# A hybrid decoder layer on one core: the merge's first two blocks interleaved, one gate half moved into attention, the sums of the down projection behind its weights

## The chip, the cores and the metric

The kernel runs on one core of one Trainium2 chip. The metric is the device time of one execution in microseconds (us). The engines are TensorE (PE for its matmuls, PEld for its weight loads), VectorE (DVE), ScalarE (ACT), GpSimd (POOL) and SyncE (SP, which here only issues DMAs; a few stores are issued on ACT's queue). Each engine runs its own instructions in a fixed order, so an instruction that waits holds everything behind it on that engine.

## What is computed

One decoder layer on x of 1024 positions x 1024 channels in float32, and a last norm:

```python
xn = rmsnorm(x, norm_mix_w)
da_q, da_k, da_v, sw_q, sw_k, sw_v, g_da, g_sw = split_cols(xn @ w_in)
y_da = diff_attention(da_q, da_k, da_v, lam, lam_init, subln_w)
y_sw = sliding_window_attention(sw_q, sw_k, sw_v, sinks)
merged = sigmoid(g_da) * (y_da @ w_br_da) + sigmoid(g_sw) * (y_sw @ w_br_sw)
x = x + merged @ w_mix_out
xn = rmsnorm(x, norm_ffn_w)
x = x + conv_ffn(xn, w_up, conv_w, conv_b, w_down)
return rmsnorm(x, norm_final_w)
```

`conv_ffn` is an up-projection to 2 x 2816 channels, a causal depthwise convolution of width 3, a SwiGLU and a down-projection. Differential attention has 4 heads of two 64-wide queries each, the sliding window (128 positions) 8 heads with sinks.

## The kernel before

Activations are held transposed: channels on the 128 partitions, positions along the free axis, in 8 tiles of 128 channels (KC = 8), the positions in two halves of 512 (H2). Every float32 operand of a product is split into a high part (a cast to fp32r on ACT, `wh`, `yh`, `mh`, `h`) and the rest (a subtraction on DVE, `wl`, `yl`, `ml`); a product is three matmuls, high x high, low x high and high x low, which are lines L153 to L155 in the helper `mm3`. Weights come in blocks of 128 output channels: `load_w` loads one (SP), casts it (L132, ACT) and subtracts (L134, DVE). `next_w` keeps two weights prepared ahead; there are three raw buffers (RAW = 3).

The order of the instructions on each engine is set by a scheduler from the program; `tc.high_priority` moves what is inside it forward, and `tc.issue_after(i)` keeps what is inside it behind the instruction i.

The stages, with their place in the profile:

- `project` (to some 247 us): the columns of `w_in` for queries, keys and values.
- `attention` (to some 488 us): six units u of eight steps of 128 queries. Units 0 to 3 are a head of differential attention each, units 4 and 5 are half of the sliding window's heads (`sw_step`). A step computes scores (L707), the softmax on DVE, ACT and DVE (L714, L716, L721), transposes (L728), a split of the transposed weights (L731 on ACT, L732 on DVE) and the product with the values, "the AV matmuls" (L738). It then copies half of the result across partitions (L740, ACT) and adds the other half (L745, DVE) into `ys`, which is stored to `yd` (L540, ACT's queue).
- Gates. The columns of `w_in` for the two gates do not belong to attention, but their matmuls fill PE between its steps. `back_half(m, hf)` does one half (512 positions) of one gate tile: 24 matmuls into a psG buffer (of two), a copy to SBUF (L548, ACT) and a store to `gd` (L549, ACT's queue). HALVES says how many halves follow which step: one tuple before attention, one for each unit, and a last one for those left over, which `rest` puts between the splits of y.
- `rest`: loads the eight tiles of y from `yd` (L763, four buffers) and splits them (L806 on ACT, L807 on DVE), with the gate halves left over between them; then the merge, 502.45 to 589.5 us. For each block m of 128 output channels: load the gate tiles of both branches (L775), multiply by the norm's factor (L776, POOL), sigmoid (L783, ACT), 24 matmuls of the differential branch into `sc`, 2 x 12 of the sliding window's into two psG buffers, DVE multiplies the gates in (L787, L792), POOL adds the branches (L793, on DVE for the last block), and the sum is split into `mh` (L796, ACT) and `ml` (L797, DVE). There are four buffers `gr` for gate tiles, two for each block, so the gate loads of block m + 2 wait for block m.
- `mix`, `hidden`: the output product of the merge, the norm, the up-projection, convolution and SwiGLU; the results c of 22 tiles go to `hd` in DRAM.
- `down` (from some 1106 us): the product with `w_down`. First 16 "pieces" over tiles 0 to 5 of the hidden channels; then a Strassen-Winograd scheme over tiles 6 to 13 with operands B11, B21, B22 and the sums T1 to T4; then tiles 14 to 21. In the scheme, step m of the first loop takes the weight of block m and multiplies it with B11 and B21 (24 matmuls, L887); the second loop multiplies the sums of weights S1 to S4 and A22 with T1, T2, B22, T3, T4. `sums_h(k)` makes the k-th tile of T1 to T4: four loads `hr` (L980), four subtractions on DVE (L996, L998, L999, L1002) and four splits (L806, L807). It has nine buffers `hr`.

Names that recur below: S is the start of the merge's first matmul; "DA(m)" and "SW(m)" are the matmuls of the two branches of block m.

Of the kernel before, what the change touches and what calls it, by code (L numbers as in the profile page):

```python
# [17 lines left out]
P = 128  # L18
D = 1024
T = 1024  # L20
KC = D // P
# [10 lines left out]
LPAD, RPAD = 480, 480  # L32
LAM_INIT = 0.2

HALVES = ((2,), (0, 0, 0, 0, 1, 0, 1, 0), (0, 0, 0, 0, 1, 0, 1, 0), (0, 0, 0, 0, 1, 0, 1, 0), (0, 0, 0, 1, 1, 0, 1, 0), (1, 0, 1, 0, 1, 0, 1, 0), (0, 0, 1, 0, 1, 0, 1, 0), (4,))
NEGMASK = 1e30


# [4 lines left out]
class Trunk:  # L43
# [652 lines left out]
    def sw_step(self, g, n, st):  # L696
        nc, ap = self.nc, self.ap
        q, k = st
        k0 = max(n - 1, 0) * P
        w = P if n == 0 else 256  # L700
        bo = T + (P if n == 0 else 0)
        sc = self.tl(self.psS, [P, 4, 256], "sc")
        s = self.tl(self.st, [P, 4, 4], "sw", bufs=4)
        L = self.tl(ap, [P, 4, 256], "L", bufs=4)
        for h in range(4):
            for part in range(2):
                nc.tensor.matmul(sc[:, h, :], q[h][:, n * P:(n + 1) * P], k[part][:, k0:k0 + 256], start=part == 0, stop=part == 1)  # L707


        a, at, we = (0, w, w + 1) if n == 0 else (1, 0, w)  # L710
        nc.gpsimd.tensor_copy(L[:, :, at:at + 1], self.nsink[:, 4 * g:4 * g + 4].unsqueeze(2))
        for h in range(4):
            slope, ns = 2.0 ** -(4 * g + h + 1), self.nsink[:, 4 * g + h:4 * g + h + 1]
            nc.vector.tensor_tensor_reduce(L[:, h, a:w], sc[:, h, a:w], self.bias[:, bo + a:bo + w], slope, ns, ALU.add, ALU.min, s[:, 0, h:h + 1])  # L714
        for h in range(4):
            nc.scalar.activation(L[:, h, :we], L[:, h, :we], AF.Exp, bias=s[:, 0, h:h + 1], scale=-1.0, accum_out=s[:, 2, h:h + 1])  # L716
        nc.vector.reciprocal(s[:, 3, :], s[:, 2, :])
        if n:
            nc.gpsimd.memset(L[:, :, 0:1], 0.0)
        for h in range(4):  # L720
            self.last = nc.vector.tensor_scalar(L[:, h, a:w], L[:, h, a:w], s[:, 3, h:h + 1], None, ALU.mult)  # L721
        po = self.tl(self.psT, [P, H2], "t")
        nblk = w // P
        parts = []
        for b in range(nblk):
            ps = self.tl(self.psT, [P, 4, P], "t")
            for h in range(4):
                nc.tensor.transpose(ps[:, h, :], L[:, h, b * P:(b + 1) * P], self.ident)  # L728
            pt = self.tl(ap, [P, 2, 4, P], "aT", F32R, bufs=5)
            hi, lo = pt[:, 0], pt[:, 1]  # L730
            nc.scalar.copy(hi, ps)  # L731
            nc.vector.tensor_tensor(lo, ps, hi.bitcast(F32), ALU.subtract)  # L732
            parts.append((hi, lo))
        for b, (hi, lo) in enumerate(parts):
            kb = k0 // P + b
            va = self.vsw[kb // 4][:, kb % 4, g]
            for m, pt in enumerate((hi, lo)):
                nc.tensor.matmul(po, va, pt, start=b == 0 and m == 0, stop=b == nblk - 1 and m == 1)  # L738
        t = self.tl(self.gpool, [P, 4, P], "g", bufs=2)[0:64]
        nc.scalar.copy(t, po[64:128].rearrange("p (h q) -> p h q", h=4))  # L740
        pv = po[0:64].rearrange("p (c e q) -> p c e q", c=2, e=2)
        tv = t.rearrange("p (c e) q -> p c e q", e=2)
        y = self.tl(ap, [P, 2, P], "ys", bufs=3)
        for e in range(2):
            nc.vector.tensor_tensor(y[64 * e:64 * e + 64], pv[:, :, e], tv[:, :, e], ALU.add)  # L745
        self.store(self.yd[4 + 2 * g:6 + 2 * g, :, n * P:(n + 1) * P].rearrange("c p q -> p c q"), y)


    def rest(self, gctx):
        nc, tc = self.nc, self.tc  # L750
        with ExitStack() as ctx:
            e = ctx.enter_context
            mctx = ExitStack()
            mh, ml = [], []
            with gctx, ExitStack() as bctx:
                yrp = bctx.enter_context(tc.tile_pool(name="yrp", bufs=4, reuse_waits="tile"))
                yp = bctx.enter_context(tc.tile_pool(name="yp", bufs=1, reuse_waits="tile"))
                bp = bctx.enter_context(tc.tile_pool(name="bp", bufs=2, reuse_waits="tile"))
                parts = []
                for c in range(8):  # L760
                    with tc.high_priority(200):
                        r = self.tl(yrp, [P, T], "yr")
                        nc.sync.dma_start(r, self.yd[c])  # L763
                    parts.append(self.split(*(yp.tile([P, T], F32R, name=f"y{p}{c}") for p in "hl"), r))
                    if self.back[7][0]:
                        self.back_half(*self.back[7][0].pop(0))
                yact = [lambda kc, hf, o=o: [t[:, hf * H2:(hf + 1) * H2] for t in parts[o + kc]] for o in (0, 4)]
                self.xctx.close()
                mp = mctx.enter_context(tc.tile_pool(name="mp", bufs=1, side="right", reuse_waits="tile"))
                for m in range(KC):  # L770
                    w = self.next_w()
                    gs = []
                    for br in range(2):
                        g = self.tl(bp, [P, T], "gr", bufs=4)
                        nc.sync.dma_start(g, self.gd[8 * br + m])  # L775
                        i = nc.gpsimd.tensor_tensor(g, g, self.rstd, ALU.mult)  # L776
                        if m == 0:

                            tc.add_manual_dep(i.ins, self.last.ins.name, mybir.DependencyInfo(mybir.DependencyClass.Sync, mybir.DependencyReason.DATA),
                                              reason="softmax first")  # L780

                        with tc.issue_after(self.hi.ins) if br else nullcontext():
                            nc.scalar.activation(g, g, AF.Sigmoid)  # L783
                        gs.append(g)
                    ps = self.tl(self.psS, [P, T], "sc")
                    self.mm3_both(ps, w, yact[0], range(4))
                    nc.vector.tensor_tensor(gs[0], gs[0], ps, ALU.mult)  # L787
                    for hf in range(2):
                        ps = self.tl(self.psG, [P, H2], "g")
                        self.mm3(ps, w, yact[1], hf, range(4), o=4)  # L790
                        g = gs[1][:, hf * H2:(hf + 1) * H2]
                        nc.vector.tensor_tensor(g, g, ps, ALU.mult)  # L792
                    (nc.vector if m == KC - 1 else nc.gpsimd).tensor_tensor(gs[0], gs[0], gs[1], ALU.add)  # L793
                    a = mp.tile([P, T], F32R, name=f"mh{m}")
                    b = mp.tile([P, T], F32R, name=f"ml{m}")
                    nc.scalar.copy(a, gs[0])  # L796
                    nc.vector.tensor_tensor(b, gs[0], a.bitcast(F32), ALU.subtract)  # L797
                    mh.append(a)
                    ml.append(b)

            pair = self.mix(mh, ml, mctx)
            self.hidden(pair)
            self.down()
# [231 lines left out]
    def down(self):  # L1035

        nc, tc = self.nc, self.tc
        with ExitStack() as ctx:
# [28 lines left out]
            sums = [lambda k=k: self.sums_h(k) for k in range(4)]  # L1067
            pss = {}
            n = N1 // 2
            for i, (m, c) in enumerate(self.pieces):  # L1070
# [3 lines left out]
                w = [v[:, i % 2 * n:i % 2 * n + n] for v in w2]  # L1074
# [17 lines left out]
                if i in STORE:  # L1092

                    with tc.issue_after(self.load.ins):
                        self.late.pop(0)()
                if i == len(self.pieces) - 1:
                    sums.pop(0)()
                if c == 1:

                    for hf in range(m < 4, 2):  # L1100
# [3 lines left out]
            ys = []  # L1104
            for m in range(4):
                wh, wl = self.next_w()
                y, ps = bank(1), pss[m, 0]
                ys.append(y)
                self.product(y, (wh[:, 0:4], wl[:, 0:4]), "B11", skip=True, low=True)
                self.product(ps, (wh[:, 4:8], wl[:, 4:8]), "B21", first=False)  # L1110
                for p in (y, ps):
                    tt(col(m, 0), col(m, 0), p, ALU.add)
                if sums:
                    sums.pop(0)()
            late = [(hf, j) for hf in range(2) for j in range(N1 + 8, NF)]
            for m, y in enumerate(ys):
                w = self.next_w()
# [36 lines left out]
            for hf in range(2):  # L1154
                for m in range(KC if hf == 0 else KC - 2):
                    w = self.next_w()
# [10 lines left out]
            for a, b in ((0, q), (q, H2)):  # L1167
                for m, w in ws:
                    ps = bank(m % 2)[:, :q]
                    mms(ps, w, 1, js, a, b, lambda n, m=m: tail.pop(0)() if a and n == (4 if m < KC - 1 else 2) else None)  # L1170
                    sq = evac(ps, m, 1, a, b)
# [100 lines left out]
```

## Time and profile before

| | us |
|---|---|
| median of 3 runs | 1345.15 (1344.61 to 1345.49) |
| profiled execution | 1344.88 |
| its span | 1343.0 |
| TensorE busy | 1326.8 |
| VectorE busy | 1052.5 |
| ScalarE busy | 602.3 |
| GpSimd busy | 488.8 |

The mean granted clock of TensorE was 0.997 of full speed. The profile is of one execution. Its page gives each engine's busy time as a share of the span; other views list what an engine waited for, the busy time of each engine in given stretches, and every instruction with its start, its length and, in brackets, the idle time of its engine ahead of it and what ended that. L12 is line 12 of the kernel. Matmuls are pipelined: the length shown for one is longer than the distance to the next.

### The profile page before, as it was taken

What the parts mean: (1) busy time and instruction counts of PE and PEld (TensorE: products, weight loads), DVE (VectorE), ACT (ScalarE), POOL (GpSimd) and SP (SyncE); (2) the same over time, 40 slices, a digit from 0 to 9 for tenths busy, and PEclk for the clock granted to TensorE, in tenths of its full rate; (3) what the DMA queues carried; (4) which work ended last, traced back from release to release, by engine and by line L of the source; (5) the groups of instructions that cost most, each with busy time, mean ns of one, the idle gap of its engine ahead of it and who ended that gap; (6) DMA issues with size and microseconds to landing.
All of it is one profiled execution on the core that took longest, in us unless ns stands there. A gap on an engine that the chain in (4) does not pass through costs nothing.

```text
span 1343.0 us, 17167 instructions
## 1 busy us (share of the span) xinstructions
PE 1326.8 (99%) x6304; PEld 1105.7 (82%) x6304; DVE 1052.5 (78%) x1425; ACT 602.3 (45%) x929; POOL 488.8 (36%) x364
## 2 busy tenths in 40 slices
PE   8999999999999999999999999999999999999997
PEld 6888888888888878888888888888888888788886
DVE  7846775388898976445669999999999998967454
ACT  8432232276667774344444434343434345432433
POOL 0346652000101016642446566666666611131011
PEclk9999999999999999999999999999999999999998
DMA  7244443966554245324522222222222239642342
GB/s 258 108 146 162 148 149 119 273 170 189 143 148 144 70 155 206 141 95 130 167 79 95 79 79 85 88 79 79 88 85 80 86 128 320 220 145 98 94 141 79
DMA packets 63812, 179.49 MB, mean 134 GB/s; under 512 B 7024, under 2 KB 16880, under 8 KB 63728
## 3 DMA queue, kind: packets, MB, share of 16 engines
q1 hardware_dynamic: 52272, 161.22, 36.8%
q10 hardware_dynamic: 11456, 17.18, 3.5%
q8 instruction: 50, 0.82, 0.2%
q14 instruction: 34, 0.28, 0.1%
HBM read 129.61 MB, written 48.76 MB: 133 GB/s over the span
## 4 chain that ended last, share of the span: by engine, by line
PE 72%; DVE 15%; issue 8%; DMA 2%; ACT 1%; POOL 1%; SPq 0%; POOLq 0%; DVEq 0%; ACTq 0%
PE t L887 24%; PE g L153 4%; PE g L154 4%; PE g L155 4%; DVE c L1031 3%; PE y L1056 3%; PE d L1056 3%; PE sc L154 3%; PE sc L155 3%; PE sc L153 3%; PE d L887 3%; PE sc L619 3%; PE y L887 2%; DVE wl L113 2%; DMA hr<-hd 2%
## 5 line engine op out<-in xcount | busy, mean ns | idle before, releaser
L1020 POOL TENSOR_TENSOR us<-us,rstd 128x1024 f32<-128x1024 f32 x42 | 92.6, 2225 | 85.0 <-DVE us L452 47.6
L1029 ACT ACTIVATE c<-us,vecs 128x1024 f32<-128x1024 f32 x44 | 54.8, 1248 | 118.3 <-POOL us L1020 113.8
L132 ACT CAST wh<-raw 128x1024 fp32r<-128x1024 f32 (+2 forms) x58 | 58.7, 1012 | 107.9 <-PE sc L154 35.8
L134 DVE TENSOR_TENSOR wl<-raw,wh 128x1024 fp32r<-128x1024 f32 (+2 forms) x58 | 78.3, 1352 | 32.5 <-ACT wh L132 22.8
L113 DVE TENSOR_TENSOR sl<-sf,sh 128x1024 fp32r<-128x1024 f32 x62 | 89.3, 1442 | 12.8 <-ACT sh L111 12.8
L111 ACT CAST sh<-sf 128x1024 fp32r<-128x1024 f32 x62 | 64.5, 1042 | 61.6 <-PE t L887 44.0
L97 POOL TENSOR_TENSOR sf<-rv 128x512 f32<-128x512 f32 x30 | 51.3, 1711 | 93.6 <-DVE sl L113 51.1
L1031 DVE SCALAR_TENSOR_TENSOR c<-us,vecs,c 128x1024 f32<-128x1024 f32 x44 | 75.4, 1746 | 2.7 <-ACT c L1029 2.7
L99 POOL TENSOR_TENSOR sf<-raw,rv 128x512 f32<-128x512 f32 x30 | 56.7, 1891 | 46.3 <-DVE sl L113 46.3
L1032 DVE SCALAR_TENSOR_TENSOR c<-us,vecs,c 128x1024 f32<-128x1024 f32 x44 | 73.2, 1696 | 0.0
L153 PE MATMUL g<-xh,wh 128*128 128x512 f32 x176 | 71.0, 403 | 1.5 <-ACT g L548 1.5
L154 PE MATMUL g<-xl,wh 128*128 128x512 f32 x176 | 70.3, 400 | 0.0
L155 PE MATMUL g<-xh,wl 128*128 128x512 f32 x176 | 70.3, 399 | 0.0
L170 POOL TENSOR_TENSOR rs<-ms,mhalf 128x8 f32<-128x8 f32 (+2 forms) x9 | 13.5, 1499 | 155.5 <-DVE ms L168 149.4
L1012 ACT ACTIVATE c<-c 128x1024 f32<-128x1024 f32 x22 | 23.4, 1064 | 89.6 <-DVE c L1032 89.6
L113 DVE TENSOR_TENSOR wl<-raw,wh 128x1024 fp32r<-128x1024 f32 (+1 forms) x35 | 61.8, 1765 | 0.3 <-ACT wh L111 0.2
L602 POOL MEMSET aT<- 128x128 f32 x32 | 6.1, 204 | 151.5 <-PE t L648 101.2
L623 DVE CUSTOM_DVE_ANT_0 L<-sc,bias 128x128 f32<-128x128 f32 (+7 forms) x64 | 47.8, 752 | 16.6 <-PE sc L619 13.7
L98 POOL TENSOR_TENSOR sf<-sf,raw 128x512 f32<-128x512 f32 x31 | 58.2, 1877 | 2.2
L624 ACT ACTIVATE L<-L,sm 128x128 f32<-128x128 f32 (+7 forms) x64 | 49.6, 778 | 20.0 <-DVE sm L623 17.3
L776 POOL TENSOR_TENSOR gr<-gr,rstd 128x1024 f32<-128x1024 f32 x16 | 40.3, 2523 | 43.9 <-DMA gr<-gd 43.7
L113 DVE TENSOR_TENSOR wl<-rv,wh 128x512 fp32r<-128x512 f32 x30 | 54.0, 1800 | 2.6 <-ACT wh L111 2.6
(435 smaller groups left out, 4338.4 us busy)
## 6 DMA issues: line engine op xcount, KB each, us to landing
u<-qd SPq DMA_DIRECT2D x72, 256.0 KB, 6.4
raw<-in_w_down SPq DMA_DIRECT2D x27, 512.0 KB, 3.7
hr<-hd SPq DMA_DIRECT2D x50, 256.0 KB, 4.8
raw<-in_w_up SPq DMA_DIRECT2D x23, 512.0 KB, 3.5
raw<-in_w_in SPq DMA_DIRECT2D x22, 512.0 KB, 3.8
hd<-c SPq DMA_DIRECT2D x22, 512.0 KB, 2.6
rv<-in_w_up SPq DMA_DIRECT2D x21, 512.0 KB, 3.5
gr<-gd SPq DMA_DIRECT2D x16, 512.0 KB, 3.4
```

The lines of the kernel that those rows point to most:

```text
L111: cast = nc.scalar.copy(hi, src)
L113: low = nc.vector.tensor_tensor(lo, src, hi.bitcast(F32), ALU.subtract)
L132: self.hi = nc.scalar.copy(wh, raw)
L134: self.lo = (eng or nc.vector).tensor_tensor(wl, raw, wh.bitcast(F32), ALU.subtract)
L153: nc.tensor.matmul(ps, wh[:, kc + o, :], ah, start=first and n == 0, stop=False)
L154: nc.tensor.matmul(ps, wh[:, kc + o, :], al, start=False, stop=False)
L155: nc.tensor.matmul(ps, wl[:, kc + o, :], ah, start=False, stop=last and n == len(kcs) - 1)
L887: nc.tensor.matmul(ps, (ah, ah, al)[p][:, k, :], (bh, bl, bh)[p], start=first and n == p == 0, stop=last and p == 2 and n == len(ks) - 1, ...
L1020: i = (nc.vector if m % NF == 0 else nc.gpsimd).tensor_tensor(us[:, 2:], us[:, 2:], self.rstd, ALU.mult)
L1031: nc.vector.scalar_tensor_tensor(c, us[:, 1:T + 1], cw[1], c, ALU.mult, ALU.add)
L1032: nc.vector.scalar_tensor_tensor(c, us[:, 0:T], cw[0], c, ALU.mult, ALU.add)
L1056: nc.tensor.matmul(ps, v[:, n, :], x, start=n == i == 0, stop=n == len(js) - 1 and i == 2)
```

## The change

1. HALVES: one half gate more in unit 5 (after its first step), one less at the end (3 instead of 4).
2. `sw_step`: the tile that receives the copy L740 is no longer taken from the gates' pool (`gpool`, tag "g", two buffers, which the gate copies L548 use too) but from attention's own pool (tag "sq", one buffer, which `da_norm` uses for its squares).
3. The merge's loop body is cut in two: `first(m)` has the weight, the gates and DA(m) with L787, `second(m)` has SW(m) and everything after it. The calls run first(0), first(1), second(0), second(1), first(2), second(2), first(3) and so on.
4. `down`: `sums_h(0)` was called after the last piece, and `sums_h(k + 1)` after the products of step m = k. Now `sums_h(m)` is called in step m after `next_w`, ahead of the products, and is kept behind the cast of the weight that `next_w` prepared last (`self.hi`).

```diff
--- before.py
+++ after.py
@@ -32,7 +32,7 @@
 LPAD, RPAD = 480, 480
 LAM_INIT = 0.2
 
-HALVES = ((2,), (0, 0, 0, 0, 1, 0, 1, 0), (0, 0, 0, 0, 1, 0, 1, 0), (0, 0, 0, 0, 1, 0, 1, 0), (0, 0, 0, 1, 1, 0, 1, 0), (1, 0, 1, 0, 1, 0, 1, 0), (0, 0, 1, 0, 1, 0, 1, 0), (4,))
+HALVES = ((2,), (0, 0, 0, 0, 1, 0, 1, 0), (0, 0, 0, 0, 1, 0, 1, 0), (0, 0, 0, 0, 1, 0, 1, 0), (0, 0, 0, 1, 1, 0, 1, 0), (1, 0, 1, 0, 1, 0, 1, 0), (1, 0, 1, 0, 1, 0, 1, 0), (3,))
 NEGMASK = 1e30
 
 
@@ -736,7 +736,7 @@
             va = self.vsw[kb // 4][:, kb % 4, g]
             for m, pt in enumerate((hi, lo)):
                 nc.tensor.matmul(po, va, pt, start=b == 0 and m == 0, stop=b == nblk - 1 and m == 1)
-        t = self.tl(self.gpool, [P, 4, P], "g", bufs=2)[0:64]
+        t = self.tl(ap, [P, 4, P], "sq", bufs=1)[0:64]
         nc.scalar.copy(t, po[64:128].rearrange("p (h q) -> p h q", h=4))
         pv = po[0:64].rearrange("p (c e q) -> p c e q", c=2, e=2)
         tv = t.rearrange("p (c e) q -> p c e q", e=2)
@@ -767,7 +767,7 @@
                 yact = [lambda kc, hf, o=o: [t[:, hf * H2:(hf + 1) * H2] for t in parts[o + kc]] for o in (0, 4)]
                 self.xctx.close()
                 mp = mctx.enter_context(tc.tile_pool(name="mp", bufs=1, side="right", reuse_waits="tile"))
-                for m in range(KC):
+                def first(m):
                     w = self.next_w()
                     gs = []
                     for br in range(2):
@@ -785,6 +785,9 @@
                     ps = self.tl(self.psS, [P, T], "sc")
                     self.mm3_both(ps, w, yact[0], range(4))
                     nc.vector.tensor_tensor(gs[0], gs[0], ps, ALU.mult)
+                    return m, w, gs
+
+                def second(m, w, gs):
                     for hf in range(2):
                         ps = self.tl(self.psG, [P, H2], "g")
                         self.mm3(ps, w, yact[1], hf, range(4), o=4)
@@ -797,6 +800,13 @@
                     nc.vector.tensor_tensor(b, gs[0], a.bitcast(F32), ALU.subtract)
                     mh.append(a)
                     ml.append(b)
+
+                todo = []
+                for m in range(KC):
+                    todo.append(first(m))
+
+                    while len(todo) > (m == 0):
+                        second(*todo.pop(0))
 
             pair = self.mix(mh, ml, mctx)
             self.hidden(pair)
@@ -1093,8 +1103,6 @@
 
                     with tc.issue_after(self.load.ins):
                         self.late.pop(0)()
-                if i == len(self.pieces) - 1:
-                    sums.pop(0)()
                 if c == 1:
 
                     for hf in range(m < 4, 2):
@@ -1104,14 +1112,15 @@
             ys = []
             for m in range(4):
                 wh, wl = self.next_w()
+
+                with tc.issue_after(self.hi.ins):
+                    sums.pop(0)()
                 y, ps = bank(1), pss[m, 0]
                 ys.append(y)
                 self.product(y, (wh[:, 0:4], wl[:, 0:4]), "B11", skip=True, low=True)
                 self.product(ps, (wh[:, 4:8], wl[:, 4:8]), "B21", first=False)
                 for p in (y, ps):
                     tt(col(m, 0), col(m, 0), p, ALU.add)
-                if sums:
-                    sums.pop(0)()
             late = [(hf, j) for hf in range(2) for j in range(N1 + 8, NF)]
             for m, y in enumerate(ys):
                 w = self.next_w()
```

## The prediction

> **What bounds the kernel now.** I read the table of engines first, then what TensorE (PE) waited for, then the stages of the edits.
>
> ```profile
> span 1343.0 us, 17167 instructions
> PE 1326.8 (99%) x6304; PEld 1105.7 (82%) x6304; DVE 1052.5 (78%) x1425; ACT 602.3 (45%) x929; POOL 488.8 (36%) x364
> PE t L280 <- ACT wh L310: 5.0, 1, 5.0
> PE g L153 <- ACT g L548: 1.5, 4, 0.5
> PE y L887 <- DVE wl L134: 0.5, 1, 0.5
> PE t L738 <- DVE aT L732: 0.4, 1, 0.4
> PE y L887 <- ACT wh L132: 0.3, 1, 0.3
> PE d L1083 <- DVE wl L134: 0.2, 1, 0.2
> PE t L728 <- DVE ys L745: 0.2, 1, 0.2
> ```
>
> The first two lines are the page's top, the rest the list of PE's waits (total us, times, longest). PE is busy 99% of the span: the kernel is bound by matmuls, and the change neither adds nor removes one. It can only win or lose waits, and those that it can reach are few. The biggest, 5.0 us, is at the kernel's start and not touched. The stages of the edits, by windows (us, PE busy, PEld, DVE, ACT, POOL busy, PEclk, DMA share, GB/s):
>
> ```profile
> 450.00:486.00 36.00, 34.40 (x187) 27.81 (x187) 33.46 (x106) 26.72 (x74) 1.96 (x9) 1.00 0.26 80
> 486.00:502.45 16.45, 16.45 (x74) 13.48 (x73) 9.50 (x9) 10.97 (x14) 4.80 (x2) 1.00 0.58 202
> 502.45:589.50 87.05, 87.05 (x386) 72.10 (x385) 44.79 (x39) 34.32 (x35) 57.90 (x21) 1.00 0.45 164
> 1164.00:1180.00 16.00, 15.24 (x67) 11.96 (x66) 15.90 (x25) 7.01 (x10) 0.00 (x0) 1.00 0.73 240
> ```
>
> The end of attention (to 486) has 36.00 - 34.40 = 1.60 us of idle PE, the start of the last part of `down` 0.76. The gates left over (to 502.45) and the merge (to 589.5) have none: there the change can only lose. The granted clock is 1.00 in all four.
>
> **What a wait costs.** Matmuls are pipelined, so a wait costs more than the idle time shown. From PE's timeline (start, length; in brackets the idle time ahead and what ended it):
>
> ```profile
> 411.36 0.50 PE L153 MATMUL g<-xh,wh 128*128 128x512 f32 x1 [0.25 <-ACT g L548]
> 411.69 0.39 PE L154 MATMUL g<-xl,wh 128*128 128x512 f32 x1
> 502.45 0.39 PE L153 MATMUL sc<-yh,wh 128*128 128x512 f32 x1
> 589.49 0.39 PE L153 MATMUL sc<-mh,wh 128*128 128x512 f32 x1
> ```
>
> The last two rows bound the merge: 8 blocks x 48 matmuls in 87.04 us, so 0.227 us from start to start, although each is shown 0.39 long. Idle time is thus counted only 0.16 us after the next could have started, and the first after a wait takes 0.33 instead of 0.23 (411.36 to 411.69). I add 0.26 us to each wait. A gate half of 24 matmuls is 5.44 us, a merge block 10.88.
>
> **Part 1: a half gate into the last unit, and tiles of its own.** A gate's matmuls (L153) need a psG buffer, which the ACT copy L548 empties. Rows of the timeline:
>
> ```profile
> 461.70 0.50 PE L153 MATMUL g<-xh,wh 128*128 128x512 f32 x1 [0.35 <-ACT g L548]
> 473.55 0.50 PE L153 MATMUL g<-xh,wh 128*128 128x512 f32 x1 [0.39 <-ACT g L548]
> 482.13 1.19 PE L738 MATMUL t<-aT,v 128*128 128x512 f32 x4 [0.37 <-DVE aT L732]
> 423.06 0.63 PE L728 MATMUL t<-ident,L 128*128 128x128 f32 x4 [0.18 <-DVE ys L745]
> 483.36 0.58 ACT L740 COPY g<-t 64x512 f32<-64x512 f32 x1 [1.52 <-PE t L738]
> 483.97 0.58 ACT L548 COPY g<-g 128x512 f32<-128x512 f32 x1
> 484.61 0.50 PE L153 MATMUL g<-xh,wh 128*128 128x512 f32 x1 [0.50 <-ACT g L548]
> 487.91 0.58 ACT L740 COPY g<-t 64x512 f32<-64x512 f32 x1 [1.51 <-DMA yd<-ys]
> ```
>
> At 483.36 the step's copy L740 waits 1.52 us for its AV matmul L738 (PE), with L548 queued behind it on ACT; PE then needs what L548 frees. The step's copy sits in the gates' own pool of two, so each can also wait for the other's consumer or store (the row at 487.91). With tiles of their own and one more half, the instruction order of the changed kernel puts each L548 of this stretch mostly ahead of the step's L740, at least 7 us of PE work (some 30 matmuls) before its buffer is used again. So the four waits should go: 0.25 + 0.35 + 0.39 + 0.50 + 4 x 0.26 = 2.5 us (bounds 0 to 2.5). The waits of L738 and L728 (0.37 + 0.18 + 2 x 0.26 = 1.07) have more gate matmuls to fill them, but DVE is busy 33.46 of 36.00 us here, so late DVE work may stay late: I take half, 0.5 (bounds 0 to 1.07). Part 1: -3.0. The new tile shares its one buffer with attention's squares; their last reader, the column sums after unit 3, precedes it in the order, and between steps only DVE's L745 holds it: nothing.
>
> The moved half takes its store L549 and the cast and split of its weight with it, on queues that precede the merge anyway. What it leaves is cover: after the last AV matmul 46 gate matmuls remain (10.4 us), 65 before (14.7). That cover hides the store of the last step and the reload and split of y, which the merge needs.
>
> **Part 2: merge's first two blocks together.** PE now runs DA(0), a part of SW(0), DA(1), the rest of SW(0), SW(1), then blocks as before. This answers the shorter cover: counting matmuls in the new order, the last y part is needed at S + 8.6 us (S: the merge's first matmul, 502.45 before), against S + 7.5 before. But the second block's weight is needed at S + 9.75, against S + 10.9. Rows of DVE and POOL at this place, and of POOL's chain:
>
> ```profile
> 505.25 2.44 DVE L807 TENSOR_TENSOR yl<-yr,yh 128x1024 fp32r<-128x1024 f32 x2 [0.69 <-ACT yh L806]
> 507.61 3.44 DVE L134 TENSOR_TENSOR wl<-raw,wh 128x1024 fp32r<-128x1024 f32 x1
> 506.66 6.65 POOL L776 TENSOR_TENSOR gr<-gr,rstd 128x1024 f32<-128x1024 f32 x2 [12.90 <-DMA gr<-gd]
> 514.37 2.40 POOL L793 TENSOR_TENSOR gr<-gr,gr 128x1024 f32<-128x1024 f32 x1 [1.05 <-ACT wh L132]
> 526.33 3.37 POOL L793 TENSOR_TENSOR gr<-gr,gr 128x1024 f32<-128x1024 f32 x1
> 568.20 4.86 POOL L776 TENSOR_TENSOR gr<-gr,rstd 128x1024 f32<-128x1024 f32 x2 [3.45 <-DMA gr<-gd]
> 573.03 3.37 POOL L793 TENSOR_TENSOR gr<-gr,gr 128x1024 f32<-128x1024 f32 x1
> 584.68 3.38 POOL L793 TENSOR_TENSOR gr<-gr,gr 128x1024 f32<-128x1024 f32 x1
> 595.11 1.23 DVE L797 TENSOR_TENSOR ml<-gr,mh 128x1024 fp32r<-128x1024 f32 x1
> 599.01 0.39 PE L153 MATMUL sc<-mh,wh 128*128 128x512 f32 x1
> ```
>
> *The second weight.* Its split L134 ended at 511.05, S + 8.6. It took 3.44 us beside POOL's L776, a y split ahead of it half of 2.44. In the changed order SyncE's queue has a fourth weight load ahead of block 0's gate loads, so POOL's four L776 of the first two blocks come in one run around S, among four y splits and this L134. If the y splits end by S + 7.6 and L134 then waits for one L776, it ends near S + 11; if for two, at S + 12.4: 2.6 us late; if for none, S + 8.8: in time. I take +0.8 (bounds 0 to 2.6).
>
> The Trainium skill (SBUF — State Buffer, "Who interferes with whom") says that a DVE instruction with two SBUF inputs and a GpSimd instruction that reads SBUF block each other for the whole instruction. The 3.44 us above agree; by that rule every L776 that meets a split costs its full length, and this term would be its bound, 2.6, and the sum 1343.2.
>
> *POOL's chain.* POOL takes per block 3.45 (the gate load, released by the last sum) + 4.86 (two L776) + 3.37 (L793) = 11.7 us, as 573.03 to 584.68 shows, more than PE's 10.88: it falls behind by 0.8 a block. Its end is the last split (595.11 + 1.23 = 596.34), of which PE's first use is at 599.01 (mh, with ml one matmul later): slack 2.9. After the change SW(0) ends after 72 matmuls, S + 16.3, instead of S + 10.9, so L793(0) comes 5.4 later and ends at about S + 19.6. But in the order L793(1) then stands behind one L776 instead of two: 19.6 + 3.45 + 2.4 + 3.4 = S + 28.8, against (526.33 + 3.37 - 502.45) = S + 27.2 before. The chain runs 1.6 us later, within the slack of 2.9: nothing (bounds 0 to 5.4 - 2.9 = 2.5).
>
> **Part 3: the sums of `down` behind the weights.**
>
> ```profile
> 1167.08 2.40 ACT L806 CAST h<-hr 128x512 fp32r<-128x512 f32 x4 [4.48 <-DVE hr L999]
> 1169.39 1.04 ACT L132 CAST wh<-raw 128x1024 fp32r<-128x1024 f32 x1
> 1170.48 2.11 PE L887 MATMUL y<-h,wh 128*128 128x512 f32 x8 [0.30 <-ACT wh L132]
> 1171.77 1.23 DVE L134 TENSOR_TENSOR wl<-raw,wh 128x1024 fp32r<-128x1024 f32 x1
> 1173.05 1.20 PE L887 MATMUL y<-h,wl 128*128 128x512 f32 x4 [0.45 <-DVE wl L134]
> ```
>
> The second weight's cast waits on ACT behind four casts of the sums, which waited 4.48 us for DVE; its split waits behind the sums on DVE; PE waits for both. In the new order this cast and this split stand ahead of the sums: 0.30 + 0.45 + 2 x 0.26 = 1.27 us go (bounds 0 to 1.27). No instruction is added. What becomes late is the sums: on SyncE the loads of the third and fourth now stand behind two or three weight loads, which wait for free weight buffers. The fourth sum's first part is due in the S1 T1 product, some 22 us after the first product; DVE's order holds its split behind PE's fourth y product, some 3 us before that, and DVE was full here (15.90 of 16.00). I take nothing (bounds 0 to one step of 24 matmuls, 5.4, less 1.5 of slack: 3.9). The wait at L1083 (0.2) lies before all of this and stays.
>
> **Sum.** Profiled execution 1344.88 (span 1343.0 and 1.9 around it; 0.27 under the median 1345.15): 1344.88 - 3.0 + 0.8 - 1.27 = 1341.4.
>
> **Rivals.**
> - *All waits go, none comes* (L1083's 0.2 + 0.26 too): 1344.88 - 2.5 - 1.07 - 1.27 - 0.5 = 1339.5. For it: the slacks above. Against it: DVE's load in both stretches.
> - *The merge's second weight is late in full:* 1344.88 - 3.0 - 1.27 + 2.6 = 1343.2. For it: 3.44; against it: the y splits beside POOL took 1.22 each.
> - *The change does not do what it says in attention:* the waits move from L548 to the aT chain, as DVE is 93% busy: 1344.88 - 1.27 + 0.8 = 1344.4. Against it: 24 more filler matmuls among the same DVE work.
> - *The sums hold the T1 product* (+3.9): 1344.88 - 3.0 + 0.8 - 1.27 + 3.9 = 1345.3. Against it: DVE's order above.
> - *Slower: POOL's chain ends the merge.* L793(0) keeps its 5.4, and each pair of L776, now out of step with DVE's pauses, grows by what L793 has against its undisturbed row (3.37 to 2.40, 1.0 us) over six blocks: 5.4 + 6.0 - 2.9 = 8.5 at the mix, so 1344.88 - 3.0 - 1.27 + 8.5 = 1349.1. For it: no slack in a cycle longer than PE's. Against it: only the first two blocks change. It decides from a chain 2.9 late, and makes the kernel slower from about 10 late.
>
> **How the numbers follow.** A measurement of this kernel can tell about 0.2% (2.7 us: below 1342.5, above 1347.8) from no change. Forecast 0.46 (1341.4, its own range 1339.5 to 1343.0; 0.42 faster, 0.04 same), all gone 0.10 (faster), late second weight 0.13 (0.02 faster, 0.11 same), attention unmoved 0.10 and late sums 0.05 (same), POOL's chain 0.16 (slower). Faster 0.54, same 0.30, slower 0.16. The range 1339.0 to 1347.0 leaves out the slow case and a little below.
>
> **What would show it.** Right: no wait of L153 for L548; the window that ends attention with under 0.8 us of idle PE; no wait for ACT wh L132 or DVE wl L134 at L887; L793's starts still 11.7 apart. Wrong: PE waits for DVE wl L134 or yl some 9 us into the merge; the mix waits for mh or ml; L887 waits for DVE h L807 of a sum, or the waits of L738 grow. A kernel over 1347.8 with the attention waits gone would mean that a slack of part 2 or 3 was misjudged.

## The result and the profile after

The changed kernel takes 1347.49 us (median of 14 runs, 1346.20 to 1349.72), the kernel before 1344.52 (14 runs). The ratio is 1.0023, interval 1.0015 to 1.0031: slower by 3.0 us where a gain of 3.5 was forecast, and above the range by 0.5. The profiled execution is 1346.99, its span 1345.2 to 1343.0 before.

PE's waits in the changed kernel, in the list of before (us in total, times, longest), and the windows of the edited stages, cut at the merge's first matmul and the mix's first:

```profile
PE t L280 <- ACT wh L310: 4.9, 1, 4.9
PE sc L155 <- DVE wl L134: 1.5, 1, 1.5
PE sc L154 <- DVE ml L800: 0.5, 2, 0.3
PE g L153 <- DVE gr L795: 0.5, 1, 0.5
PE sc L153 <- ACT wh L132: 0.2, 1, 0.2
PE sc L154 <- DVE yl L817: 0.2, 1, 0.2
PE d L897 <- DVE h L817: 0.2, 1, 0.2
```

```profile
450.00:486.00 36.00, 36.00 (x199) 29.82 (x197) 33.21 (x110) 26.24 (x75) 1.68 (x10) 1.00 0.24 76
500.44:591.36 90.92, 88.46 (x385) 71.69 (x384) 52.18 (x40) 34.05 (x34) 56.90 (x22) 1.00 0.42 148
591.36:604.00 12.64, 12.10 (x52) 9.35 (x51) 7.70 (x9) 3.83 (x5) 2.45 (x1) 1.00 0.27 84
1164.00:1180.00 16.00, 16.00 (x72) 13.27 (x71) 15.41 (x23) 8.84 (x14) 0.00 (x0) 1.00 0.65 206
```

The rows of L153 for L548 are gone, and so are both of L887 at the start of `down`: the end of attention has no idle PE at all (1.60 before). In their place the merge and the start of the mix, which had no wait, have six. Measured from matmul start to matmul start, attention's first score to S takes 244.7 us (247.0 before), S to the mix's first matmul 90.9 (87.0), the mix 88.0 (86.8), the stretch of `down` from the first matmul of its Strassen-Winograd scheme to the first of its tail loop 76.8 (77.5). So attention wins 2.3 and `down` 0.7; the merge loses 3.9 and the mix 1.2. The other stages differ by 0.1 to 0.3 us. (Each kernel has one profile, and places that no edit touches differ too: in the eighteen profiles attention's first score starts at 254.6 to 256.1 us, and PE's wait at L1083 in `down`, 0.24 us before, is anything from none to 1.4.) The six waits, from PE's timeline:

```profile
503.07 0.50 PE L154 MATMUL sc<-yl,wh 128*128 128x512 f32 x1 [0.20 <-DVE yl L817]
509.28 0.50 PE L153 MATMUL sc<-yh,wh 128*128 128x512 f32 x1 [0.21 <-ACT wh L132]
512.93 0.50 PE L155 MATMUL sc<-yh,wl 128*128 128x512 f32 x1 [1.54 <-DVE wl L134]
585.78 0.50 PE L153 MATMUL g<-yh,wh 128*128 128x512 f32 x1 [0.51 <-DVE gr L795]
596.21 0.50 PE L154 MATMUL sc<-ml,wh 128*128 128x512 f32 x1 [0.35 <-DVE ml L800]
602.14 0.50 PE L154 MATMUL sc<-ml,wh 128*128 128x512 f32 x1 [0.19 <-DVE ml L800]
```

The first three are at the merge's start, the fourth is in its last block and the last two are in the mix. What stood around the start (DVE, POOL and SyncE's issues, a row with x2 or more covering several):

```profile
490.88 0.33 SPq L122 DMA_DIRECT2D raw<-in_w_br  x1
491.31 0.88 SPq L775 DMA_DIRECT2D gr<-gd  x2
494.74 8.62 SPq L763 DMA_DIRECT2D yr<-yd  x4
496.17 5.76 POOL L776 TENSOR_TENSOR gr<-gr,rstd 128x1024 f32<-128x1024 f32 x2 [10.61 <-DMA gr<-gd]
496.77 9.65 DVE L817 TENSOR_TENSOR yl<-yr,yh 128x1024 fp32r<-128x1024 f32 x5 [0.92 <-ACT yh L816]
508.31 1.23 DVE L817 TENSOR_TENSOR yl<-yr,yh 128x1024 fp32r<-128x1024 f32 x1 [1.90 <-ACT yh L816]
508.51 6.64 POOL L776 TENSOR_TENSOR gr<-gr,rstd 128x1024 f32<-128x1024 f32 x2 [6.58 <-DMA gr<-gd]
509.46 3.42 DVE L134 TENSOR_TENSOR wl<-raw,wh 128x1024 fp32r<-128x1024 f32 x1
```

Block 0's gate loads are issued at 491.31, behind a weight load (490.88); before it was 483.39:

```profile
483.39 4.87 SPq L775 DMA_DIRECT2D gr<-gd  x2
```

POOL's L776 so falls among the y splits: five take 9.65 us, 1.93 each, where one is 1.23 alone. The last y load waits for a buffer that such a split frees (the issue row runs from 494.74 to 503.36), its split ends at 509.5, and then L134 of the second weight meets the next L776: 3.42 us. PE waits for all three.

### The profile page after: what moved, and what is told of

Its sections match the earlier page's. It is cut to its first block, busy times and chain, and to the rows that moved or that the text cites. A ratio compares the mean times of both kernels' runs of the same rounds, so it can differ in the third digit from the quotient of the medians.

```text
span 1345.2 us, 17173 instructions
## 1 busy us (share of the span) xinstructions
PE 1327.4 (99%) x6304; PEld 1103.5 (82%) x6304; DVE 1064.1 (79%) x1425; ACT 602.3 (45%) x929; POOL 487.5 (36%) x364
## 4 chain that ended last, share of the span: by engine, by line
PE 89%; DVE 3%; DMA 3%; POOL 3%; issue 1%; ACT 1%; SPq 0%; POOLq 0%; DVEq 0%; ACTq 0%
PE t L897 44%; PE y L1066 3%; PE d L1066 3%; PE g L154 3%; PE g L153 3%; PE g L155 3%; PE sc L619 3%; PE d L1093 2%; PE y L1093 2%; PE d L897 2%; PE sc L155 2%; PE sc L154 2%; PE sc L153 2%; DMA gr<-gd 2%; POOL gr L796 2%; PE y L897 2%
## 5 line engine op out<-in xcount | busy, mean ns | idle before, releaser
L134 DVE TENSOR_TENSOR wl<-raw,wh 128x1024 fp32r<-128x1024 f32 (+2 forms) x58 | 81.5, 1407 | 31.4 <-ACT wh L132 21.6
L113 DVE TENSOR_TENSOR sl<-sf,sh 128x1024 fp32r<-128x1024 f32 x62 | 90.4, 1459 | 10.9 <-ACT sh L111 10.9
L97 POOL TENSOR_TENSOR sf<-rv 128x512 f32<-128x512 f32 x30 | 47.2, 1574 | 95.3 <-DVE sl L113 52.1
L153 PE MATMUL g<-xh,wh 128*128 128x512 f32 x176 | 70.6, 401 | 0.0
L1022 ACT ACTIVATE c<-c 128x1024 f32<-128x1024 f32 x22 | 23.4, 1064 | 89.6 <-DVE c L1042 89.6
L776 POOL TENSOR_TENSOR gr<-gr,rstd 128x1024 f32<-128x1024 f32 x16 | 41.3, 2583 | 39.1 <-DMA gr<-gd 39.1
```

What stands on the lines that cost most here:

```text
L113: low = nc.vector.tensor_tensor(lo, src, hi.bitcast(F32), ALU.subtract)
L134: self.lo = (eng or nc.vector).tensor_tensor(wl, raw, wh.bitcast(F32), ALU.subtract)
L153: nc.tensor.matmul(ps, wh[:, kc + o, :], ah, start=first and n == 0, stop=False)
```

## The experiments

Each ran in 5 rounds (5 to 12 executions) beside the kernel before, whose medians in the four sets were 1345.05, 1344.99, 1344.95 and 1344.87. "Attention" is attention's first score to S, "merge" S to the mix's first matmul, "mix" from there to its last, all by matmul starts in the profiled execution.

| | median us | ratio, interval | attention | merge | mix |
|---|---|---|---|---|---|
| before | 1344.52 | | 247.0 | 87.0 | 86.8 |
| changed | 1347.49 | 1.0023, 1.0015 to 1.0031 | 244.7 | 90.9 | 88.0 |
| attn_only | 1344.17 | 0.9995, 0.9986 to 1.0004 | 244.7 | 87.9 | 87.9 |
| merge_only | 1350.36 | 1.0040, 1.0027 to 1.0053 | 247.2 | 92.1 | 88.4 |
| sums_only | 1345.46 | 1.0009, 1.0001 to 1.0018 | 247.1 | 87.0 | 86.8 |
| no_merge | 1345.00 | 1.0004, 0.9995 to 1.0012 | 244.8 | 87.0 | 87.9 |
| w1_before_pool | 1345.08 | 1.0005, 0.9997 to 1.0014 | 244.7 | 87.8 | 87.5 |
| gates_early | 1344.07 | 1.0001, 0.9992 to 1.0010 | 244.6 | 88.0 | 87.5 |
| no_merge_gates_early | 1343.77 | 0.9993, 0.9984 to 1.0002 | 244.7 | 88.4 | 87.5 |
| w1_first | 1346.38 | 1.0013, 1.0004 to 1.0022 | 244.7 | 90.2 | 87.6 |
| attn_gates_early | 1345.41 | 1.0000, 0.9991 to 1.0009 | 244.9 | 89.6 | 87.7 |
| half_only | 1345.11 | 0.9998, 0.9989 to 1.0007 | 245.2 | 88.1 | 86.8 |
| tile_only | 1349.22 | 1.0032, 1.0019 to 1.0044 | 244.1 | 94.6 | 86.8 |
| sum_on_dve | 1342.72 | 0.9983, 0.9975 to 0.9992 | 244.6 | 87.0 | 86.8 |
| before_sum_on_dve | 1344.74 | 0.9999, 0.9990 to 1.0008 | 247.1 | 87.0 | 86.8 |
| after_sum_on_dve | 1345.10 | 1.0003, 0.9994 to 1.0012 | 244.7 | 89.7 | 86.8 |
| part1_sums_dve | 1341.70 | 0.9975, 0.9965 to 0.9985 | 244.7 | 87.6 | 86.8 |
| after_repaired | 1342.95 | 0.9986, 0.9977 to 0.9995 | 244.7 | 88.0 | 86.8 |

**The parts alone.** The hunks of the change's diff, taken one at a time or with one left out: attn_only has HALVES and the tile, merge_only `first` and `second`, sums_only the sums in step m, and no_merge all but `first` and `second`; half_only and tile_only, further down, have one line of attn_only each:

```diff
-HALVES = (..., (0, 0, 1, 0, 1, 0, 1, 0), (4,))
+HALVES = (..., (1, 0, 1, 0, 1, 0, 1, 0), (3,))
-        t = self.tl(self.gpool, [P, 4, P], "g", bufs=2)[0:64]
+        t = self.tl(ap, [P, 4, P], "sq", bufs=1)[0:64]
```

> Only part 1 (half gate moved, tile of its own); merge and sums as before. Queue theory (with a half gate less at the end, the fourth merge weight's load passes block 0's gate loads on SyncE; these land 8 us later, so POOL's L776 run among the y splits, and the y splits come late): the merge starts about 2 us earlier, but PE waits some 0.5 us for the fourth y split and 1 to 2 us for the last one, which here is due earlier than in the changed kernel: about 1344.3, no change. Interleaving theory (all of the merge's loss comes from taking two blocks together): no wait in the merge, the 2.2 us of attention stay won: 1342.3.

> Only the merge's new order; attention and sums as before. Queue theory: block 0's gate loads stay early (483), so no wait for y splits and none for the second weight; what is left is POOL's chain, whose L793(0) comes 5.4 us later: 0 to 1 us of waits at the mix, 1344.5 to 1345.5. Interleaving theory: the changed kernel's 4.6 us of waits between 500 and 603 us all appear: about 1349.

> Only the sums of down moved. As in the changed kernel: the two waits before the second weight (1.3 us) go, one of 0.45 us for a fourth sum's split h appears: 1343.7. A rival, that this late wait hangs on the earlier stages' timing, has no such wait: 1343.2.

> Parts 1 and 3 without the merge's new order. Queue theory: as attn_only, less 0.8 for the sums: about 1343.5. Interleaving theory: attention's 2.2 and the sums' 0.8 both stay won: 1341.5.

The queue theory, as I first had it, fell: merge_only keeps the gate loads early and has no late y split, and yet loses most of these four. Its second weight and the wait for it:

```profile
507.77 3.39 DVE L134 TENSOR_TENSOR wl<-raw,wh 128x1024 fp32r<-128x1024 f32 x1
511.21 0.51 PE L155 MATMUL sc<-yh,wl 128*128 128x512 f32 x1 [2.40 <-DVE wl L134]
```

Taking two blocks together asks for the second weight earlier, and PE waited 2.40 us for an L134 that again ran 3.39 us beside L776; some 1.5 us more followed in a slow clock (last section). merge_only is not the changed kernel's merge by itself, though: the scheduler's order has PE reach this weight's low part after 28 matmuls of the merge here, after 42 in the changed kernel.

Without the new order no_merge's merge takes its 87.0 us again. But attn_only and no_merge do not keep attention's 2.3: 1.0 to 1.1 us of it is lost in the mix, and in attn_only 0.8 in the merge. So the interleaving theory does not hold as a whole either. attn_only's forecast of 1344.3 came out (1344.17) by luck: the 1 to 2 us of waiting for the last y split did not come, and the 1.1 us lost in the mix were not in it. sums_only and no_merge, forecast 1343.7 and 1343.5, took 1345.46 and 1345.00. Gain and loss are told apart by the stages better than by the medians, which scatter by about 1 us. The late wait for a sum was there in sums_only (0.4 us), as in the changed kernel.

**The second weight and POOL.** First the order of POOL behind the weight, or of the weight ahead of y, in the changed kernel:

```diff
w1_before_pool:
                     w = self.next_w()
+                    if m == 0:
+                        self.w1 = self.lo
...
                         i = nc.gpsimd.tensor_tensor(g, g, self.rstd, ALU.mult)
+                        if m == 1:
+                            tc.add_manual_dep(i.ins, self.w1.ins.name, ...)
w1_first:
-                    w = self.next_w()
+                    with tc.high_priority(200) if m == 0 else nullcontext():
+                        w = self.next_w()
```

> The changed kernel, but POOL's two L776 of block 1 wait for the split L134 of the second weight. Lock theory (PE's 1.7 us at the second weight come from this L134 meeting L776, 3.4 us long instead of 1.2): L134 ends near S + 10.2, before PE needs it, the wait for DVE wl goes, and as L793(0) is set by PE, POOL's chain is no later: about 1345.7. Lateness theory (the y splits ahead of it are late by themselves, because the last y load is): the wait stays at 1 us or more, 1347.

> The changed kernel, but the second weight is cast and split ahead of the last four tiles of y, so PE has DA(0) and DA(1) before it needs these. Both theories of the start: the wait for wl L134 goes (1.8 us). Lateness theory: a wait for the last y splits of up to 1 us takes its place. POOL's chain is late as before, so the waits at 586, 596 and 602 (1.9 us) stay: 1345.5 to 1346.5.

With L776 of block 1 held back, the three waits at the start are gone and the time is 2.4 us under the changed kernel's. DVE and POOL of w1_before_pool:

```profile
507.86 1.22 DVE L134 TENSOR_TENSOR wl<-raw,wh 128x1024 fp32r<-128x1024 f32 x1
509.16 4.77 POOL L778 TENSOR_TENSOR gr<-gr,rstd 128x1024 f32<-128x1024 f32 x2 [5.97 <-DVE wl L134]
```

The same split, 1.22 us instead of 3.42, and two L776 in 4.77 instead of 6.64: each had slowed the other. In this execution the y splits ahead were also 1.2 us earlier (L134 started 7.8 us after S, not 9.0). So the split ended 3.4 us earlier against S, of which 2.2 are its own length beside L776, the lock of the forecast, and 1.2 the y splits. w1_first, 1346.38, lies within its forecast of the time, but was a miss in part: the weight's wait went, and a wait of 1.4 us for the last y split, not of up to 1, took its place.

**The gate loads.** Block 0's gate loads back ahead of the later weights, with the merge's new order, without it, and without the sums' move:

```diff
-                    w = self.next_w()
+                    with tc.issue_after(self.gload.ins) if m == 1 else nullcontext():
+                        w = self.next_w()
...
-                        nc.sync.dma_start(g, self.gd[8 * br + m])
+                        self.gload = nc.sync.dma_start(g, self.gd[8 * br + m])
```

> The changed kernel with block 0's gate loads ahead of the third and fourth weight's loads on SyncE. Queue theory, now only for the y splits: L776 of block 0 runs before the y splits again, yl[3] and the second weight's cast are in time (0.47 and 0.48 us go), the last y load is issued 2 us earlier, the wait for the second weight shrinks to under 0.5: about 1345. Lock theory alone: block 1's L776 still meets L134, its 1.7 us stay: about 1346.5.

> Parts 1 and 3 without the merge's new order, block 0's gate loads ahead of the third and fourth weight's. Queue theory: POOL's chain starts some 2 us earlier than without this, the two waits of the mix for ml (0.98 us with their refill) go, the span is 1340.8 and the time 1344.0. If the lateness of POOL's chain came from elsewhere, the two waits stay and the time is that of no_merge, 1345.0.

> Part 1 alone, with block 0's gate loads ahead of the third and fourth weight's; merge and sums as before. If the sums' move costs time in some executions, as its slow tail says, this is no_merge_gates_early without that: 1343.2, no execution over 1347. If the sums' move is worth its 0.7 us of the profile: 1344.4.

gates_early has no wait at the merge's start, L134 takes 1.22, and it is 3.4 us under the changed kernel. Here L134 started 8.1 us after S, not 9.0, and ended at 509.5, just ahead of the next L776 (509.68): both the lateness and the meeting are gone, so this run does not tell them apart. (Its profiled execution, 1347.79, is one of the slowest of its eleven and has the wait of 2.27 us in `down` of the last section; its median is 1344.07.)

no_merge_gates_early took 1343.77, close to the 1344.0 of its first theory, but not for its reason: the waits at the merge's end did not go (two of 0.7 us in all for the multiply that empties psG, 0.2 for ml), and there its time should have been 1345.0. attn_gates_early has them too (1.5 us in two waits, 0.2 for ml), so late gate loads of block 0 were not what that end waited for; at 1345.41 it lies above both of its forecasts.

**The two lines of part 1.**

> Only the half gate moved; the step's copy stays in the gates' pool. If the filler alone makes the copies L548 early, the four waits of L153 for L548 go and the merge starts 2 us earlier; then the time is that of attn_only, 1344.2. If the shared pool holds them, two or more of the four waits stay, the start comes 0.5 to 1 us earlier, and with the shorter cover the time is 1345 to 1346.

> Only the step's copy in a tile of its own; the halves as before. If the shared pool caused the waits, they go without the moved half, the merge starts 2 us earlier with its full cover, and the merge and the mix have no wait: 1343. If it is the filler, the four waits stay: 1345.

The tile alone takes all four waits of L548 and 2.9 us; the half alone three of the four and 1.9. Either is nearly enough in attention; half_only's 1345.11 has a wait of 0.56 us for the second weight. The forecast for tile_only was right in attention and wrong by 6 us in sum. The order that the scheduler made for it puts the second weight's L134 ahead of the last y split, and both met L776:

```profile
505.13 3.42 DVE L134 TENSOR_TENSOR wl<-raw,wh 128x1024 fp32r<-128x1024 f32 x1
508.47 3.35 DVE L807 TENSOR_TENSOR yl<-yr,yh 128x1024 fp32r<-128x1024 f32 x1
505.00 5.74 POOL L776 TENSOR_TENSOR gr<-gr,rstd 128x1024 f32<-128x1024 f32 x2 [3.28 <-DMA gr<-gd]
511.88 0.79 PE L154 MATMUL g<-yl,wh 128*128 128x512 f32 x1 [4.72 <-DVE yl L807]
```

**POOL's chain.** The add of the two branches on DVE for blocks 4 to 7: on attn_gates_early, on the kernel before, on the changed kernel, and with the sums; and last on w1_before_pool, which keeps the whole change.

```diff
-                    (nc.vector if m == KC - 1 else nc.gpsimd).tensor_tensor(gs[0], gs[0], gs[1], ALU.add)
+                    (nc.vector if m >= 4 else nc.gpsimd).tensor_tensor(gs[0], gs[0], gs[1], ALU.add)
```

> As attn_gates_early, and the add of the two branches (L793) on DVE instead of POOL for blocks 4 to 7. Chain theory (what part 1 wins is partly given back because POOL's chain, 11.7 us a block to PE's 10.9, now ends the merge): the waits from 570 to 600 (1.5 us with their refill) go, and the time is 1.5 under attn_gates_early, about 1341.7. Rival: DVE, which then has four more instructions, becomes late itself and the waits only change their name: as attn_gates_early.

> The kernel before with the add of the two branches on DVE for blocks 4 to 7, and nothing else. Chain theory: before, POOL's chain ends inside its slack of 2.9 us and no wait hangs on it, so moving it wins nothing: 1345.0. Rival (the DVE add is a gain of its own, whatever part 1 does): 1343 or less.

> The changed kernel with the add on DVE for blocks 4 to 7. Chain theory: the waits at the merge's end and in the mix (1.9 us with their refill) go, the 2.7 at its start stay: 1345.6. If the late chain only follows the late start: 1347.

> sum_on_dve (part 1, early gate loads, add on DVE) with the sums moved as well. If the sums' move is worth the 1.3 us of waits that it takes from the start of its loop: 1341.5 to 1342. If what it takes is given back by late sums and, in some executions, a long wait: 1342.7 or more, with executions over 1345.

> The whole change, with POOL's L776 of block 1 behind the second weight's split and the add on DVE for blocks 4 to 7. Lock and chain theory together: neither the 1.8 us at the second weight nor the waits at the merge's end are left, at most 0.5 at its start: 1342.0 to 1343.0, the same as part1_sums_dve: taken together or not, the first two blocks then cost the same. If the new order has a cost of its own: 1344 or more.

The chain theory held in every one. With L793 of the last blocks taken out of the chain, the waits at the merge's end and in the mix are gone (the mix is 86.8 in all five rows of the table), and it is worth nothing in the kernel before, which has no such waits. sum_on_dve is 2.7 us under attn_gates_early, more than the 1.5 forecast. The merge of sum_on_dve, to be read against 502.45 to 589.50 of before:

```profile
499.98:587.01 87.03, 87.03 (x385) 72.07 (x384) 52.12 (x42) 33.79 (x34) 48.46 (x18) 1.00 0.49 174
```

POOL is busy 48.5 us instead of 57.9, DVE 52.1 instead of 44.8, and PE has no idle time. after_repaired, the whole change with its two losses repaired, is 1.9 us faster than the kernel before, within its forecast (1342.95). But it is 1.2 over part1_sums_dve, where the same was expected: its merge still has 1.0 us more than before (a wait of 0.7 for a y split), and in its profile a sum is 1.2 us late in `down` (0.2 in part1_sums_dve). The merge's new order wins nothing here against the old one; what part of the 1.2 is its own is not shown, as the two kernels also differ in how the start is repaired. The fastest, part1_sums_dve at 0.9975 of before, has parts 1 and 3, the early gate loads and the add on DVE, and the merge in its old order.

## Why the prediction was wrong, point by point

*The signs.* Three of the four signs of being right came true: no wait for L548, no idle PE in the window that ends attention, no wait for the weight at L887. The fourth, adds of POOL still 11.7 us apart, did not, and three signs of being wrong came too: PE waiting for the second weight and a y split in the merge, the mix waiting for ml, a product waiting for a sum.

*Part 1.* Right in mechanism: the four waits went, and those of L738 and L728 with them. It gave 2.3 us instead of 3.0. tile_only, which has none of these six waits and no new one, gains 2.9, so all six were worth 2.9 and not the 3.6 of the prediction (2.5 + 1.07); and in the changed kernel a new one (L728 for the softmax's L721, 0.24 idle) came at 486.45. The shorter cover was named and not priced. By itself it does not set the loss: the last AV matmul is followed by 46 gate matmuls in attn_only and by 55 in tile_only, and the merge loses 0.8 in the one and 7.6 in the other, where the second weight and the last y split both meet L776.

*The second weight.* This step failed in size. "I take +0.8 (bounds 0 to 2.6)": the wait was 1.54 idle, 1.8 with its refill (the 0.26 us that the prediction adds to each wait), and two more that the sum had no term for, the fourth y split and the second weight's cast, cost 0.5 each; together 2.8. L134 ended at S + 12.4, the prediction's latest case, but by another way: not after y splits that end by S + 7.6 and then two L776, but after y splits that ended at S + 9.1, and 2.2 us longer beside L776. The prediction saw the fourth weight load ahead of the gate loads, and the run of L776 that it makes around S, but put a price only on L134 and not on the y splits and on the y load behind them. What it held against the late weight, y splits of 1.22 beside POOL, was misread: of the two in that row (505.25 to 507.69) the first had ended and the second had begun before L776 started (506.66). The five among L776 in the changed kernel took 1.93 each. The rule of the Trainium skill (SBUF — State Buffer, "Who interferes with whom") that it set beside the row, with 2.6, was nearer, and w1_before_pool agrees with it for L134: 3.42 beside L776, 1.22 without. That the 2.6 is so close to the 2.8 of three waits is luck.

*POOL's chain.* This step failed in kind. "The chain runs 1.6 us later, within the slack of 2.9: nothing." The 1.6 is right as far as it was followed. In the changed kernel L793(0) ends 8.3 us later against S than before (at 523.07 and 516.77) and L793(1) 4.4; PE's own waits in the merge's first blocks hide 2.8 of this, which leaves 5.5 and 1.6, as forecast (5.4 and 1.6). But the prediction stopped at block 1. The L776 that no longer stands ahead of L793(1) stands ahead of L793(2), with two more. POOL of the changed kernel:

```profile
528.74 3.38 POOL L796 TENSOR_TENSOR gr<-gr,gr 128x1024 f32<-128x1024 f32 x1
532.07 2.42 POOL L776 TENSOR_TENSOR gr<-gr,rstd 128x1024 f32<-128x1024 f32 x1
535.75 2.41 POOL L776 TENSOR_TENSOR gr<-gr,rstd 128x1024 f32<-128x1024 f32 x1 [1.27 <-DMA gr<-gd]
540.00 2.39 POOL L776 TENSOR_TENSOR gr<-gr,rstd 128x1024 f32<-128x1024 f32 x1 [1.83 <-DMA gr<-gd]
542.35 3.37 POOL L796 TENSOR_TENSOR gr<-gr,gr 128x1024 f32<-128x1024 f32 x1
590.43 3.38 POOL L796 TENSOR_TENSOR gr<-gr,gr 128x1024 f32<-128x1024 f32 x1
```

From one add (L796 is the line of L793 here) to the next 13.6 us instead of 11.7. POOL's last add ends 93.4 us after S, 85.6 before: 7.8 later. Less the same 2.8, the chain is 3.5 us late at block 2 and 5.0 at its end. That exceeds the slack of 2.9, and the three waits at the end cost 1.9 with their refill.

The slack itself was also wrong once part 1 works, though the changed kernel, whose L793(0) waits for PE, does not show it. It was taken against S, as if POOL's chain came earlier with S. But the chain hangs on gate loads and y splits that follow attention's last store. In no_merge, where the blocks run in their old order, L793(0) starts straight behind block 1's L776:

```profile
509.03 5.18 POOL L776 TENSOR_TENSOR gr<-gr,rstd 128x1024 f32<-128x1024 f32 x2 [5.09 <-DMA gr<-gd]
514.16 3.39 POOL L793 TENSOR_TENSOR gr<-gr,gr 128x1024 f32<-128x1024 f32 x1
```

It ended 2.5 us later against S than before (517.55 less 500.77, to 516.77 less 502.45), and the mix waited for ml:

```profile
592.53 0.50 PE L154 MATMUL sc<-ml,wh 128*128 128x512 f32 x1 [0.25 <-DVE ml L797]
598.46 0.50 PE L154 MATMUL sc<-ml,wh 128*128 128x512 f32 x1 [0.19 <-DVE ml L797]
```

*Part 3.* The two waits went, as forecast (1.27); "I take nothing" for the sums was wrong by a wait of 0.18 to 1.2 us at the T1 product (0.18 at 1192.18 in the changed kernel), and the stretch is 0.7 us shorter instead of 1.27. Whether the move gains in time stays open: four pairs of medians with and without it give +0.4, +0.8, -1.6 and -1.0, the last two between sets that ran at different times.

*The rivals.* The outcome was two of them at once: the second weight late in full, and POOL's chain ending the merge. Each was priced with the rest of the sum intact. The range should have let them fall together: 1344.88 - 3.0 - 1.27 + 2.6 and 2.5 for the chain's bound is 1345.7, and with the 1.0 of the y split and the cast 1346.7, near the profiled execution's 1346.99. (That nearness is in part luck: parts 1 and 3 gave 1.3 us less than this sum takes, and the waits of part 2 cost 1.4 less.) The two do not need each other or part 1: merge_only has both with attention as it was, and no_merge has the chain's waits without the second weight's.

## What to carry to other kernels

Where a stage is made shorter, the next stage's slack shrinks for all that hangs on loads and other engines and does not come earlier with it (no_merge: S came earlier, L793(0) did not): take each slack against those, not against the start of the stage. A chain on another engine with a longer period than PE's (11.7 to 10.9 us here) is the bound as soon as its head start is spent, and shortening it then lets the first change's gain through (sum_on_dve). Follow such a chain to its end: here the first two links came as forecast, and the loss came behind them. Read the order after the change on every queue for what now meets: here one weight load ahead of two gate loads put GpSimd's work beside VectorE's. The scheduler makes that order anew for every edit, so a part tried alone is not quite the part in the whole (tile_only, merge_only).

## What the runs showed of the hardware

A wait of PE can cost more than its length. After the waits of 2.40 us (merge_only), 4.72 (tile_only) and 2.27 (gates_early, in `down`) PE's granted clock fell to about half, and matmuls started 0.43 us apart instead of 0.23; after the changed kernel's 1.54 it did not. Windows of merge_only, tile_only, gates_early and the changed kernel, each behind its wait (the figures are the window's length, busy PE, PEld, DVE, ACT and POOL, then the clock, where 1.00 is full speed):

```profile
512.60:516.20 3.60, 3.60 (x11) 2.81 (x10) 0.00 (x0) 0.00 (x0) 0.81 (x1) 0.55 0.32 129
```

```profile
512.60:517.00 4.40, 4.40 (x12) 3.42 (x11) 1.04 (x2) 0.00 (x0) 0.00 (x0) 0.50 0.03 10
```

```profile
1211.50:1214.90 3.40, 3.40 (x10) 2.63 (x9) 0.47 (x1) 0.33 (x1) 2.56 (x2) 0.52 0.53 202
```

```profile
513.00:517.00 4.00, 4.00 (x18) 3.31 (x19) 1.60 (x2) 0.00 (x0) 2.15 (x1) 1.00 0.45 131
```

In merge_only and in gates_early eight starts are late by 0.2 us each, some 1.5 in all; in tile_only twelve, 2.5. The Trainium skill (TensorE: Matmul & The Clock Gate, "HAM oscillation — how this bites in real kernels") warns of idle gaps above about 3.4 us; here 2.3 us was enough in one place and 1.5 was not. Whether it hangs on the wait's length or on where it falls was not tried.
